# A two-layer encoder trunk on one core: seven products per couple of weight blocks in the mixers' output projections too, a fifth such couple in the down projections, and sums of weights formed by adding transfers

## The chip, the cores and the metric

The kernel runs on one core of one Trainium2 chip. The metric is the device time of one execution in microseconds (us); before the change it is 2400.95 us, the median of three runs (2400.9 to 2401.26).

## The reference, cut to what matters

All arrays are float32. A sequence of 256 tokens with 2048 features goes through two layers. Each layer adds a mixer's result to the residual stream `h`, and then that of a gated feed-forward part (ConvGLU); a last normalisation closes the trunk.

```python
for layer in range(2):
    hn = rmsnorm(h, norm_mix_g[layer])
    mix = mlstm_mixer(...) if layer == 0 else hgrn_mixer(...)   # each ends with:  y @ w_out   (2048 x 2048)
    h = h + mix
    h = h + conv_glu(rmsnorm(h, norm_ffn_g[layer]), ...)
return rmsnorm(h, final_g)

def conv_glu(hn, w_up, conv_w, conv_b, w_down):
    a, v = jnp.split(hn @ w_up, 2, axis=-1)      # w_up 2048 x 11008
    c = conv_b + depthwise convolution of width 3 of a
    return (gelu(c) * v) @ w_down                # w_down 5504 x 2048
```

What the change touches are the products with `w_out` (both mixers) and with `w_down` (both layers).

## The kernel before, in words

**Products in three terms.** A float32 weight block is split into a high part `wh`, cast by ScalarE (`parts`, L133), and a remainder `wl = raw - wh` by VectorE (L134); the tokens' factor is kept in two such parts as well. One block product is the sum of three matmuls: high by high, high by low, low by high. Each has 128 rows of the contraction and 512 columns, and accumulates into a bank of the matmuls' memory. Weights come in as tiles `raw` of 1 MB on SyncE's queue, three buffers deep; `stream` fetches pieces (`wh`, `wl`, 1024 columns) three ahead of their use (`LOOK`), with four buffers each (`WB`).

**Chunks.** The work is a list of `Chunk`s that TensorE takes one after another: "fm" chunks (up projections and the like), "tm" chunks (512 output columns, 16 or 21 contraction tiles, two banks of the pool `psm`, line L320), and "st" chunks (`squares_by_seven`, line L214), which cover 1024 output columns at once with four banks of `psm` (`mm`) and four of `psa` (`pc`).

**Seven products instead of eight.** An "st" chunk takes the contraction tiles two at a time: a unit, or couple, is a 2 x 2 grid of token blocks A (halves of the tokens by contraction tile) times a 2 x 2 grid of weight blocks B (contraction tile by columns): eight block products, 24 matmuls. For the units listed in `SEVEN = (1, 3, 5, 7)` a Winograd form is used with seven block products, 21 matmuls. It needs four sums of token blocks (`token_sums`, from tiles of the activations, kept as `sx`) and four sums of weight blocks: `combine` forms `T` (1024 columns wide, one VectorE instruction, L184) and `T_` (two instructions of 512, L186 and L187), then the high parts `th` (ScalarE, L189) and remainders `tl` (VectorE, L190). `T` and `T_` lie in the two buffers of the tag `avc`; `th` and `tl` have one buffer each. Four products of the seven read `th` and `tl`. When the last such unit is done, `mid` distributes the shared partial products to `h` (`hm`); at the chunk's end `done` adds the four `pc` banks.

**Where st chunks stand.** Each layer's feed-forward part has two parts of 22 and 21 contraction tiles. The first part ends with two st chunks (columns 0 to 1023, then 1024 to 2047), the second with one st chunk and two tm chunks. That makes three st chunks a layer, six in all, with four units of seven products each. The mixers' output projections are four tm chunks each (`project`, c = 0 to 3).

**Order.** A scheduler fixes every engine's order when the kernel is built, so matmuls of one unit may stand between those of another. Small jobs (transposes, head computations) are queued in `side` and are emitted as the matmuls tick by. `Norm.turn` transposes finished columns of `hm` for the next normalisation; it takes banks of `psa`. At the start TensorE runs 56 matmuls on ones (`idle`, L1096) while the first transfers are under way.

Of the kernel before, what the change touches and what calls it, by code (L numbers as in the profile page):

```python
# [20 lines left out]
FA = 22  # L21
# [24 lines left out]
LEAD = 48  # L46
GATES = 4 * AH
SEVEN = (1, 3, 5, 7)

QUAD = 32  # L50
# [6 lines left out]
def trunk_kernel(ctx, tc, xT, x_d, fg_d, pp_d, cst_d, w_gate, w_first, w_aq, w_ak, w_av, w_ao, w_aout,  # L57
                 w_bq, w_bv, w_bg, w_bout, w_up, w_d0, w_d1, w_d2, out, mscr):
# [53 lines left out]
    side = Side()  # L112
# [56 lines left out]
    def split_squares(ch, parts):  # L169

        units, raws, sums = (ch.nk + 1) // 2, {}, {}

        def raw(u):
            if u not in raws and u < units:
                raws[u] = load_raw(ch.src, 2048 * u, min(2048 * (u + 1), 1024 * ch.nk))
            return raws.get(u)

        def combine(u):
# [5 lines left out]
            dve.tensor_tensor(T.rearrange("p (a b) -> p a b", a=2), B12.unsqueeze(1).broadcast_to([P, 2, 512]),  # L184
                              r[:, 0:1024].rearrange("p (a b) -> p a b", a=2), ALU.subtract)
            dve.tensor_tensor(T_[:, 0:512], B22, T[:, 0:512], ALU.subtract)  # L186
            dve.tensor_tensor(T_[:, 512:1024], B21, T_[:, 0:512], ALU.subtract)  # L187
            for c, t in ((slice(0, 1024), T), (slice(1024, 2048), T_)):
                act.copy(th[:, c], t)  # L189
                dve.tensor_tensor(tl[:, c], t, th[:, c].bitcast(F32), ALU.subtract)  # L190
# [12 lines left out]

    def squares_by_seven(ch, fetch, ready):
# [4 lines left out]
        begun = set()  # L209

# [13 lines left out]
        for u in range(units):  # L224
# [26 lines left out]
            for ps, (x, w), (y, v) in ((C11, (A11, B11), (A12, B21)), (C12, (A11, B12), (A12, B22)),  # L251
                                       (C21, (A21, B11), (A22, B21)), (C22, (A21, B12), (A22, B22))):
                product(ps, x, w, False)
                product(ps, y, v, end)
                side.tick(1.3)
        ch.done(psa_)
# [88 lines left out]
    class Norm:  # L345
# [26 lines left out]
        def turn(self, c):  # L372
            yield 2.5
            for k0 in (4 * c, 4 * c + 2):
                pz = aux("pz")
                for k in (k0, k0 + 1):
                    for t in range(2):
                        o = (k - k0) * T + t * P
                        pe.transpose(pz[:, o:o + P], hm[:, t, k * P:(k + 1) * P], ident)  # L379
                for k in (k0, k0 + 1):  # L380
                    self.take(k, pz[:, (k - k0) * T:(k - k0 + 1) * T])
                yield 1.0
            if c == 3:
                self.total()
                self.finish()
                self.spread()
# [108 lines left out]
    def slot(j, name, more=None):  # L495
        where = keep if j < KT else more
        return where.tile([P, 2 * T], F32R, tag=f"yt{j}", name=f"{name}{j}")


    def mlstm(norm, nxt):  # L500
# [273 lines left out]
        def end():  # L774
            side.drain()
            stack.close()

        tail = project(lambda c: w_aout[c], KT, yx, nxt)
        tail[1].before = end
        return chunks + tail  # L780


    def hgrn(norm, nxt):
# [197 lines left out]
        def end():  # L981
            side.drain()
            stack.close()

        tail = project(lambda c: w_bout[c], KT, yx, nxt)
        tail[1].before = end
        return chunks + tail


    def ffn(layer, norm, nxt):  # L990
# [11 lines left out]

        def token_sums(u, a, b, S, SX):

            sx = box["mp"].tile([P, 1024], F32R, tag=f"sx{SEVEN.index(u)}", name="sx")
            for i, (x, y, op) in enumerate(((a[:, P:T], b[:, P:T], ALU.add), (a[:, P:T], a[:, 0:P], ALU.subtract),
                                            (S[:, 0:P], a[:, 0:P], ALU.subtract), (b[:, 0:P], S[:, 2 * P:3 * P], ALU.subtract))):
                dve.tensor_tensor(S[:, i * P:(i + 1) * P], x, y, op)
            act.copy(sx[:, 0:512], S)
            dve.tensor_tensor(sx[:, 512:1024], S, sx[:, 0:512].bitcast(F32), ALU.subtract)  # L1010
            SX[u] = sx

        def pair(src, nk, q, GT, SX, norm):

            u = []

            def part(t, c):
                o = 1024 * q + 512 * c
                return hm[:, t, o:o + 512]

            def mid(ps):
                P1, P6, P7, P5 = ps
                u2, u3 = (box["mp"].tile([P, 512], F32, tag=n, name=n) for n in ("u2", "u3"))
                act.copy(u2, P1)
                dve.tensor_tensor(part(0, 0), part(0, 0), P1, ALU.add)
                dve.tensor_tensor(u2, u2, P6, ALU.add)
                dve.tensor_tensor(u3, u2, P7, ALU.add)  # L1027
                dve.tensor_tensor(part(1, 1), part(1, 1), P5, ALU.add)
                dve.tensor_tensor(u2, u2, P5, ALU.add)
                pool.tensor_tensor(part(1, 0), part(1, 0), u3, ALU.add)  # L1030
                pool.tensor_tensor(part(1, 1), part(1, 1), u3, ALU.add)
                pool.tensor_tensor(part(0, 1), part(0, 1), u2, ALU.add)

            def done(ps):
                for i in range(4):
                    h = part(i // 2, i % 2)
                    dve.tensor_tensor(h, h, ps[i], ALU.add)
                if norm is not None:
                    norm.add(2 * q)
                    side.push(second())  # L1040

            def second():
                yield 3.0
                norm.add(2 * q + 1)

            ch = Chunk("st", src, nk, lambda k: GT[k], done)
            ch.mid, ch.seven, ch.sums = mid, SEVEN, lambda u: SX[u]
            pairs.append(ch)
            return ch

        def done_up(f, i, GT, SX):
            def go(ps):
# [15 lines left out]
                if i % 2 and i // 2 in SEVEN:  # L1068
                    token_sums(i // 2, box["c"], c, avc[:, 0:2 * T], SX)
# [3 lines left out]
        for part, (f0, nf) in enumerate(((0, FA), (FA, FB))):  # L1073
            GT, SX = [], {}
            for i in range(nf):
                chunks.append(Chunk("fm", w_up[layer, f0 + i], KT, norm.x, done_up(f0 + i, i, GT, SX),
                                    begin if f0 + i == 0 else None,
                                    swap=(1 + (layer == 0),) if part and i == 0 else ()))
            chunks.append(pair(w_d0[layer][:, f0 * 1024:(f0 + nf) * 1024], nf, 0, GT, SX, nxt if part else None))
# [4 lines left out]
            else:  # L1084
                chunks.append(pair(w_d1[layer], nf, 1, GT, SX, None))
# [8 lines left out]
    for i in range(56):  # L1094
        o = i % 4 * QUAD
        pe.matmul(idle[o:o + QUAD, 0:86], ones[:, 0:QUAD], ones[:, 0:86], start=True, stop=True)  # L1096
# [46 lines left out]
def layout(x, norm_mix_g, norm_ffn_g, mlstm_w_in, mlstm_b_gate, mlstm_head_g, mlstm_w_out, hgrn_w_in, hgrn_lb,  # L1143
# [8 lines left out]
    def squares(q, n):  # L1152

        v = down[:, :n, :, 2 * q:2 * q + 2]
        m = n // 2
        w = v[:, :2 * m].reshape(2, m, 2, P, 2, 512)
        w = np.stack([w[:, :, 0, :, 0], w[:, :, 1, :, 1], w[:, :, 1, :, 0], w[:, :, 0, :, 1]], axis=3)
        w = w.transpose(0, 2, 1, 3, 4).reshape(2, P, m * 2048)
        return np.ascontiguousarray(np.concatenate([w, v[:, 2 * m:].transpose(0, 2, 1, 3, 4).reshape(2, P, -1)], axis=2))

    up = A(ffn_w_up).reshape(2, KT, P, 2, FT, P).transpose(0, 4, 2, 1, 3, 5)
# [14 lines left out]
        w_aout=_cols(A(mlstm_w_out)[0], 512),  # L1176
        w_bq=_cols(qfb, 256),
        w_bv=_cols(wb[:, 2048:4096], 512), w_bg=_cols(wb[:, 4096:6144], 512),
        w_bout=_cols(A(hgrn_w_out)[0], 512),
        w_up=np.ascontiguousarray(up).reshape(2, FT, P, KT * 256),  # L1180
        w_d0=squares(0, FT), w_d1=squares(1, FA),
# [4 lines left out]
def build(nc, ins, out_shape=(2, P, D), **kw):  # L1186
# [4 lines left out]
    with tile.TileContext(nc, schedule_with_timeline_sim=True) as tc:  # L1191
        with ExitStack() as ctx:
            trunk_kernel(ctx, tc, ap["xT"], ap["x"], ap["fg"], ap["pp"], ap["cst"], ap["w_gate"], ap["w_first"],
                         ap["w_aq"], ap["w_ak"], ap["w_av"],
                         ap["w_ao"], ap["w_aout"], ap["w_bq"], ap["w_bv"], ap["w_bg"],
                         ap["w_bout"], ap["w_up"], ap["w_d0"], ap["w_d1"], ap["w_d2"], out, mscr, **kw)
# [12 lines left out]
```

## Time and profile before

| | |
|---|---|
| median of three runs | 2400.95 us (2400.9 to 2401.26) |
| profiled execution, its own time | 2402.44 us |
| its span in the profile | 2400.6 us |
| TensorE (PE) busy | 2388.8 us, 14606 matmul records |
| VectorE (DVE) busy | 1829.0 us, 76% of the span |
| ScalarE (ACT) busy | 1260.8 us, 53% |
| GpSimd (POOL) busy | 185.5 us, 8% |
| bytes moved | 451.19 MB, mean 188 GB/s |

Matmuls overlap in the pipeline, so the mean duration of a record (389 ns) is longer than the distance from one to the next; the sums in the prediction go by the distance. A group's row gives busy time and mean of one instruction, then the idle time just before these instructions and what ended it.

### The profile page before, as it was taken

The page shows a single profiled execution, that of the slowest core. Times are in us where ns is not written, and L with a number is a line of the kernel's source. Part 1 is how long each engine was busy: PE and PEld are TensorE (multiplying, and loading weights), DVE is VectorE, ACT ScalarE, POOL GpSimd, SP SyncE. Part 2 cuts the span into 40 slices and gives each one's busy share as a digit, 9 for nine tenths or more (in the row PEclk, how much of TensorE's full clock was granted, in tenths as well). Part 3 has the DMA queues.
Part 4 walks back from the last instruction along what each step waited for, and adds up shares of the span by engine and source line. Part 5 has one row for each costly group of instructions (what it writes and reads, how often), then busy time and mean ns, then how long its engine had stood idle before and what let it go on. Part 6 is the DMA issues. An engine that isn't in the chain of part 4 may idle for free.

```text
span 2400.6 us, 37188 instructions
## 1 busy us (share of the span) xinstructions
PE 2388.8 (100%) x14606; PEld 2044.3 (85%) x14606; DVE 1829.0 (76%) x3009; ACT 1260.8 (53%) x1959; POOL 185.5 (8%) x242
## 2 busy tenths in 40 slices
PE   9999999999999999999999999999999999999998
PEld 7888888888888888888888888888888888888887
DVE  7766656777887777867898989885777788777784
ACT  7655455555544455555555555555555454444553
POOL 0100000000000000001222222210000000000000
PEclk9999999999999999999999999999999999999999
DMA  8654555555555555555555455545555555555654
GB/s 299 199 185 163 188 176 180 191 192 193 186 212 198 185 188 190 201 184 180 174 176 173 165 174 176 176 161 191 189 187 189 191 196 208 193 180 189 202 195 147
DMA packets 67679, 451.19 MB, mean 188 GB/s; under 512 B 7712, under 2 KB 8224, under 8 KB 15024
## 3 DMA queue, kind: packets, MB, share of 16 engines
q1 hardware_dynamic: 65520, 444.29, 54.4%
q0 software_dynamic: 1120, 3.21, 0.8%
q8 instruction: 114, 1.87, 0.3%
q10 hardware_dynamic: 864, 1.32, 0.2%
q14 instruction: 61, 0.50, 0.1%
HBM read 446.63 MB, written 2.16 MB: 187 GB/s over the span
## 4 chain that ended last, share of the span: by engine, by line
PE 99%; DMA 0%; issue 0%; ACT 0%; SPq 0%; DVE 0%; POOLq 0%; POOL 0%
PE mm L304 37%; PE mm L320 26%; PE mm L308 18%; PE pc L214 11%; PE mm L214 3%; PE pn L657 1%; PE py L921 1%; PE pd L871 0%; PE pz L379 0%; PE pa L871 0%; DMA raw<-in_w_first 0%; PE S L643 0%; PE pz L942 0%; PE pa L896 0%; PE pa L895 0%; PE pz L685 0%
## 5 line engine op out<-in xcount | busy, mean ns | idle before, releaser
L134 DVE TENSOR_TENSOR wl<-raw,wh 128x1024 fp32r<-128x1024 f32 (+1 forms) x846 | 1016.4, 1207 | 429.0 <-ACT wh L133 420.2
L304 PE MATMUL mm<-xt,wh 128*128 128x512 f32 x3776 | 1318.4, 395 | 0.0
L133 ACT CAST wh<-raw 128x1024 fp32r<-128x1024 f32 (+1 forms) x846 | 861.4, 1028 | 762.4 <-issue 260.2
L308 PE MATMUL mm<-xt,wl 128*128 128x256 f32 x3776 | 1049.2, 279 | 0.0
L304 PEld LDWEIGHTS mm<-xt,wh 128*128 128x128 f32 x3776 | 706.8, 188 | 162.3
L308 PEld LDWEIGHTS mm<-xt,wl 128*128 128x128 f32 x3776 | 710.3, 188 | 4.1 <-issue 0.4
L320 PE MATMUL mm<-wh,xt 128*128 128x512 f32 x1024 | 320.2, 391 | 2.0 <-ACT xt L326 1.1
L320 PEld LDWEIGHTS mm<-wh,xt 128*128 128x128 f32 x1024 | 191.5, 188 | 41.8 <-ACT xt L326 1.5
L214 PE MATMUL pc<-wh,g 128*128 128x512 f32 x704 | 225.2, 389 | 0.0
L320 PE MATMUL mm<-wl,xt 128*128 128x512 f32 x512 | 198.0, 391 | 0.0
L331 ACT COPY b<-mm 128x256 f32<-128x256 f32 x236 | 87.4, 370 | 158.8 <-PE mm L308 158.7
L214 PEld LDWEIGHTS pc<-wh,g 128*128 128x128 f32 x704 | 132.1, 188 | 27.5
L214 PE MATMUL pc<-wl,g 128*128 128x512 f32 x352 | 136.0, 389 | 0.0
L320 PEld LDWEIGHTS mm<-wl,xt 128*128 128x128 f32 x512 | 96.2, 188 | 18.9
L332 DVE TENSOR_TENSOR avc<-mm,b 128x256 f32<-128x256 f32 x172 | 72.0, 420 | 41.4 <-ACT b L331 41.3
L320 PE MATMUL mm<-wh,g 128*128 128x512 f32 x308 | 96.4, 391 | 0.0
L1030 POOL TENSOR_TENSOR hm<-hm,u 128x512 f32<-128x512 f32 x6 | 7.8, 1296 | 1015.5 <-DVE u L1027 1015.5
L320 PE MATMUL mm<-wh,yb 128*128 128x512 f32 x256 | 80.7, 393 | 0.0
L320 PE MATMUL mm<-wh,ya 128*128 128x512 f32 x256 | 80.6, 393 | 0.0
L214 PEld LDWEIGHTS pc<-wl,g 128*128 128x128 f32 x352 | 66.1, 188 | 13.6
L189 ACT CAST th<-T 128x1024 fp32r<-128x1024 f32 x48 | 49.1, 1052 | 48.7 <-DVE T L187 15.5
L337 DVE TENSOR_TENSOR avc<-avc,R 128x256 f32<-128x256 f32 x172 | 72.1, 421 | 2.8
(227 smaller groups left out, 2236.7 us busy)
## 6 DMA issues: line engine op xcount, KB each, us to landing
raw<-in_w_up SPq DMA_DIRECT2D x172, 1024.0 KB, 4.9
raw<-in_w_d SPq DMA_DIRECT2D x84, 1024.0 KB, 4.9
raw<-in_w_bq SPq DMA_DIRECT2D x48, 1024.0 KB, 5.0
raw<-in_w_ao SPq DMA_DIRECT2D x16, 1024.0 KB, 4.8
raw<-in_w_aout SPq DMA_DIRECT2D x16, 1024.0 KB, 4.8
raw<-in_w_bv SPq DMA_DIRECT2D x16, 1024.0 KB, 4.8
raw<-in_w_bg SPq DMA_DIRECT2D x16, 1024.0 KB, 4.8
raw<-in_w_bout SPq DMA_DIRECT2D x16, 1024.0 KB, 4.8
```

The costliest lines, as they stand in the source:

```text
L133: pin(act.copy(wh[:, :m], r))
L134: pin(dve.tensor_tensor(wl[:, :m], r, wh[:, :m].bitcast(F32), ALU.subtract))
L189: act.copy(th[:, c], t)
L214: pe.matmul(ps, a, b, start=id(ps) not in begun, stop=stop and i == 2)
L304: pe.matmul(ps[f], wh[:, c:c + P], x, start=k + kk == 0, stop=False)
L308: pe.matmul(ps[f][:, 0:T], wl[:, c:c + P], x[:, 0:T], start=False, stop=k + kk == ch.nk - 1)
L320: pe.matmul(ps[t], x[:, a + t * P:a + (t + 1) * P], w[:, c], start=st and i == 0, stop=sp and i == 2)
L331: act.copy(b, ps[:, T:2 * T])
L332: dve.tensor_tensor(dst, ps[:, 0:T], b, ALU.add)
L337: dve.tensor_tensor(dst, dst, R, ALU.mult)
L657: pe.matmul(pn[:, 0:258], w, v, start=(i == 0), stop=(i == len(parts) - 1))
L921: pe.matmul(py[:, c], AT[:, s if s == t else 2 + s], V[:, s, j * P:(j + 1) * P], start=(s == 0), stop=(s == 1))
```

## The change

- The mixers' output projections become three chunks instead of four: a tm chunk for columns 0 to 511, an st chunk for columns 512 to 1535 with units 2, 4 and 6 in seven products (`SEVEN_MIX`), and a tm chunk for the last 512 columns (`mixed`). The token sums of these units are formed by a job `token` that starts when the first chunk is done. The banks of `psa` are held by an st chunk, so a list `held` makes `Norm.turn` wait until it is over.
- The down projections' st chunks get a fifth unit of seven products: `SEVEN = (1, 3, 5, 7, 9)`.
- In the down projections the wide sum `T` is no longer formed by VectorE: `add_in_flight` has GpSimd's queue load 128 x 1024 into `T` and then add 128 x 512 into each half of it by two transfers that add to what is there. It is issued two units ahead. The signs of the sums are turned so that all of them are additions; `mid` loses the tiles `u2` and `u3`, uses the tile `jk` instead, and has six VectorE instructions and two of GpSimd where it had five and three.
- In the mixers (`late=True`) VectorE still forms `T`, and `combine` comes after the unit's first piece.
- The first `idle` matmuls are 65 of 74 columns instead of 56 of 86. The order of two matmuls at the start of the second feed-forward part is the same in both layers now (`swap`).
- The host lays out the middle columns of the output weights in squares (`outer`, `squares`).

```diff
-SEVEN = (1, 3, 5, 7)
+SEVEN = (1, 3, 5, 7, 9)
+SEVEN_MIX = (2, 4, 6)
...
+        def add_in_flight(u):
+
+            T, o = tile(), 2048 * u
+            pool.dma_start(T, ch.src[:, o:o + 1024])
+            for c in range(2):
+                pool.dma_start(T[:, 512 * c:512 * c + 512], ch.src[:, o + 1536:o + 2048], accum_op=ALU.add)
+            pre[u] = T
...
-            T, T_ = (ch.pool.tile([P, 1024], F32, tag="avc", bufs=2, name="T") for _ in range(2))
-            dve.tensor_tensor(T.rearrange("p (a b) -> p a b", a=2), B12.unsqueeze(1).broadcast_to([P, 2, 512]),
-                              r[:, 0:1024].rearrange("p (a b) -> p a b", a=2), ALU.subtract)
-            dve.tensor_tensor(T_[:, 0:512], B22, T[:, 0:512], ALU.subtract)
-            dve.tensor_tensor(T_[:, 512:1024], B21, T_[:, 0:512], ALU.subtract)
+            T = pre.pop(u, None)
+            if T is None:
+                T = tile()
+                dve.tensor_tensor(T.rearrange("p (a b) -> p a b", a=2), r[:, 0:1024].rearrange("p (a b) -> p a b", a=2),
+                                  B12.unsqueeze(1).broadcast_to([P, 2, 512]), ALU.add)
+            T_ = tile()
+            dve.tensor_tensor(T_[:, 0:512], B22, T[:, 0:512], ALU.add)
+            dve.tensor_tensor(T_[:, 512:1024], B21, T_[:, 0:512], ALU.add)
...
             r = raw(u)
-            if u + 1 in ch.seven:
-                combine(u + 1)
+            if not ch.late:
+                for v in (u + 1, u + 2) if u == 0 else (u + 2,):
+                    if v in ch.seven:
+                        add_in_flight(v)
+                if u + 1 in ch.seven:
+                    combine(u + 1)
             wh, wl = parts(r[:, 0:1024], 1024)
             yield wh, wl, 1
+            if u + 1 in ch.seven and ch.late:
+                combine(u + 1)
...
         def turn(self, c):
             yield 2.5
+            while held:
+                yield 1.0
...
+    def token_sums(mp, i, a, b, S):
+        sx = mp.tile([P, 1024], F32R, tag=f"sx{i}", name="sx")
+        ...
+        dve.tensor_tensor(S1, A22, A21, ALU.subtract)
+        dve.tensor_tensor(S3, A11, A21, ALU.subtract)
+        dve.scalar_tensor_tensor(S2, S1, -1.0, A11, ALU.mult, ALU.subtract)
+        dve.tensor_tensor(S4, A12, S2, ALU.add)
+        act.copy(sx[:, 0:512], S)
+        dve.tensor_tensor(sx[:, 512:1024], S, sx[:, 0:512].bitcast(F32), ALU.subtract)
...
+        def mid(ps):
+            P1, P6, P7, P5 = ps
+            u = ev.tile([P, 512], F32, tag="jk", bufs=1, name="u")
+            act.copy(u, P1)
+            dve.tensor_tensor(part(0, 0), part(0, 0), P1, ALU.add)
+            dve.tensor_tensor(u, u, P6, ALU.add)
+            dve.tensor_tensor(part(0, 1), part(0, 1), P5, ALU.subtract)
+            dve.tensor_tensor(part(0, 1), part(0, 1), u, ALU.subtract)
+            dve.tensor_tensor(part(1, 1), part(1, 1), P5, ALU.subtract)
+            dve.tensor_tensor(u, u, P7, ALU.add)
+            pool.tensor_tensor(part(1, 0), part(1, 0), u, ALU.add)
+            pool.tensor_tensor(part(1, 1), part(1, 1), u, ALU.subtract)
...
+    def mixed(w, w2, x, norm, close):
+
+        c0, _, _, c3 = project(lambda c: w[c // 3], KT, x, norm)
+        ...
+        two = pair(w2, KT, 1, x, sums, norm, SEVEN_MIX, True)
+
+        def token():
+            for i, u in enumerate(SEVEN_MIX):
+                f = two.pool.tile([P, 1024], F32, tag="avc", bufs=2, name="f")
+                for j in range(2):
+                    y = x(2 * u + j).bitcast(F32)
+                    dve.tensor_tensor(f[:, j * T:(j + 1) * T], y[:, 0:T], y[:, T:2 * T], ALU.add)
+                SX[u] = token_sums(two.pool, i, f[:, 0:T], f[:, T:2 * T], f[:, 2 * T:4 * T])
+                yield 5.0
+        ...
+        return [c0, two, c3]
...
-        tail = project(lambda c: w_aout[c], KT, yx, nxt)
-        tail[1].before = end
-        return chunks + tail
+        return chunks + mixed(w_aout, w_ao2, yx, nxt, stack.close)
...
-    for i in range(56):
+    for i in range(65):
         o = i % 4 * QUAD
-        pe.matmul(idle[o:o + QUAD, 0:86], ones[:, 0:QUAD], ones[:, 0:86], start=True, stop=True)
+        pe.matmul(idle[o:o + QUAD, 0:74], ones[:, 0:QUAD], ones[:, 0:74], start=True, stop=True)
```

More of the change, by code (lines that the diff above doesn't have):

```diff
@@ L255, in squares_by_seven @@
                 side.tick(1.3)
+        held.pop()
         ch.done(psa_)
@@ new lines, in pair, with part, done, second @@
+    def pair(src, nk, c0, x, sums, norm, seven, late=False):
+        def part(t, c):
+            o = 512 * (c0 + c)
+            return hm[:, t, o:o + 512]
+        def mid(ps):
[10 more added lines that the diff above has]
+            pool.tensor_tensor(part(1, 1), part(1, 1), u, ALU.subtract)
+        def done(ps):
+            for i in range(4):
+                h = part(i // 2, i % 2)
+                dve.tensor_tensor(h, h, ps[i], ALU.add)
+            if norm is not None:
+                norm.add(c0)
+                side.push(second())
+        def second():
+            yield 3.0
+            norm.add(c0 + 1)
+        ch = Chunk("st", src, nk, x, done)
+        ch.mid, ch.seven, ch.sums, ch.late = mid, seven, sums, late
+        return ch
@@ L979, in yx @@
             return YT[k]
[L981 to L987, printed above, removed]
+        return chunks + mixed(w_bout, w_bo2, yx, nxt, stack.close)
     def ffn(layer, norm, nxt):
@@ L1001, in begin @@
                 nxt.begin(box["mp"])
[L1003 to L1049, printed above, removed]
         def done_up(f, i, GT, SX):
@@ L1084, in ffn @@
             else:
-                chunks.append(pair(w_d1[layer], nf, 1, GT, SX, None))
+                chunks.append(two(w_d1[layer], 2, None))
         return chunks, stack.close
```

64 lines of the change are left out of this document (42 added, 22 removed).

## The prediction, made before the changed kernel was run

> **What bounds the kernel now.** I read the page's busy table and chain first, then the waits of TensorE, then the chain in order of time inside a down projection.
>
> ```profile
> PE 2388.8 (100%) x14606; PEld 2044.3 (85%) x14606; DVE 1829.0 (76%) x3009; ACT 1260.8 (53%) x1959; POOL 185.5 (8%) x242
> ...
> PE 99%; DMA 0%; issue 0%; ACT 0%; SPq 0%; DVE 0%; POOLq 0%; POOL 0%
> ```
>
> ```profile
> PE idle L1096 <- POOL ones L1089: 1.1, 1, 1.1
> PE mm L320 <- ACT xt L326: 1.1, 1, 1.1
> PE mm L320 <- ACT wh L133: 0.9, 1, 0.9
> ```
>
> TensorE is on the chain for 99% of the span, and it waits three times in all, 3.1 us, at the start. So a matmul that goes saves its full distance to the next one, and any wait that comes in costs its full length. The distance stands in a stretch of the chain (start, length, matmuls and weight loads as records of one line):
>
> ```profile
> 677.59 18.36 PE pc L214 x81
> ```
>
> 18.36 / 81 = 0.2267 us. A unit of eight products (24 matmuls) takes 5.44 us, one of seven (21) 4.76 us.
>
> The other engines are not idle around these stretches. The three st chunks of layer 0, then the mixer's second, third and fourth output chunks (columns: length, then PE, PEld, DVE, ACT, POOL busy, clock, share and rate of the transfer engines):
>
> ```profile
> 637.44:694.82 57.38, 57.38 (x254) 47.49 (x254) 50.97 (x59) 30.19 (x36) 3.80 (x3) 1.00 0.57 198
> 694.82:752.00 57.18, 57.18 (x254) 47.32 (x253) 45.84 (x50) 26.51 (x30) 3.80 (x3) 1.00 0.60 209
> 984.66:1039.07 54.41, 54.41 (x242) 45.06 (x241) 45.69 (x54) 27.88 (x34) 3.80 (x3) 1.00 0.56 197
> ```
>
> ```profile
> 330.40:352.20 21.80, 21.80 (x100) 18.01 (x99) 12.19 (x14) 10.33 (x14) 0.00 (x0) 1.00 0.52 178
> 352.20:374.00 21.80, 21.80 (x101) 18.03 (x100) 12.46 (x14) 11.23 (x16) 0.00 (x0) 1.00 0.53 174
> 374.00:396.00 22.00, 22.00 (x108) 18.42 (x108) 12.62 (x19) 11.23 (x16) 0.69 (x1) 1.00 0.55 182
> ```
>
> VectorE is 80 to 89% busy in the st chunks and 56% in the output chunks; the transfer engines are busy 0.52 to 0.60 of the time.
>
> **The matmuls that go.** One more unit in each of six st chunks and three in each of two mixers: 12 units, three matmuls fewer each, 36 x 0.2267 = 8.2 us. The built order of the changed kernel has just that: 36 matmuls of 512 columns fewer, nine more of `idle`, and all others, transposes too, in the old number. That is the whole gain to be had on the path: 2402.4 - 8.2 = 2394.2 us for the profiled execution (2400.6 of span and 1.8 around it), 2400.95 - 8.2 = 2392.8 for the median, which lies 1.5 below.
>
> **VectorE in the down projections.** Its forms, with mean ns of one behind the busy time:
>
> ```profile
> L134 DVE TENSOR_TENSOR wl<-raw,wh 128x1024 fp32r<-128x1024 f32 x802 | 987.2, 1236 | 420.7 <-ACT wh L133 412.3
> ...
> L190 DVE TENSOR_TENSOR tl<-T,th 128x1024 fp32r<-128x1024 f32 x48 | 57.4, 1219 | 4.2 <-ACT th L189 4.2
> ...
> L1063 DVE TENSOR_TENSOR avc<-avc 128x256 f32<-128x256 f32 x86 | 35.8, 416 | 1.0 <-ACT avc L1062 1.0
> ...
> L134 DVE TENSOR_TENSOR wl<-raw,wh 128x512 fp32r<-128x512 f32 x44 | 30.1, 686 | 8.3 <-ACT wh L133 7.9
> L184 DVE TENSOR_TENSOR T<-raw 128x1024 f32<-128x1024 f32 x24 | 29.3, 1219 | 3.8 <-DMA raw<-in_w_d 3.7
> ...
> L1008 DVE TENSOR_TENSOR avc<-avc 128x128 f32<-128x128 f32 x64 | 18.4, 287 | 1.1
> ...
> L186 DVE TENSOR_TENSOR T<-raw,T 128x512 f32<-128x512 f32 x24 | 16.5, 690 | 0.6
> ...
> L486 DVE TENSOR_TENSOR hm<-hm,mm 128x512 f32<-128x512 f32 x22 | 14.3, 681 | 4.1 <-PE mm L320 4.1
> ...
> L1010 DVE TENSOR_TENSOR sx<-avc,sx 128x512 fp32r<-128x512 f32 x16 | 10.9, 684 | 0.0
> ```
>
> ```profile
> L189 ACT CAST th<-T 128x1024 fp32r<-128x1024 f32 x48 | 49.1, 1052 | 48.7 <-DVE T L187 15.5 <-PE pc L214 13.4 <-issue 12.8
> ...
> L1024 ACT COPY u<-mm 128x512 f32<-128x512 f32 x6 | 3.5, 577 | 0.0
> ```
>
> A unit of seven cost VectorE 1.24 + 0.69 + 1.22 + 2 x 0.69 + 2 x 1.22 = 7.0 us before, against 2.5 for one of eight. A fifth on the old way adds 4.5 us to 51 of 57 and shortens the chunk by 0.7: it would not fit safely. Without the wide sum a unit costs 5.7: five are 28.7, six of eight are 14.8, `mid` and `done` ten times 0.68: 50.3 of 56.4 us. That fits about as before, so VectorE itself costs nothing; the cover is the pieces fetched three ahead (some 8 us of matmuls). `mid` now follows unit 9 instead of 7, with 2.7 us (21 tiles) or 5.4 us (22) of matmuls behind it; the next chunk wants the first two `mm` banks, free after one copy and two additions, 0.58 + 2 x 0.68 = 1.9 us. Nothing again; up to 1 us each of six times if VectorE is behind.
>
> **The chain of adding transfers.** This is the new thing, and no row shows an adding transfer. `T` keeps one buffer in the built order, and its next load waits for the remainder `tl` of the last `T`. So there is a loop: GpSimd issues the load of 512 KB, waits until it has landed, issues two adding transfers of 256 KB, these land, ScalarE casts, VectorE subtracts, and only then the next load is issued. Bounds for the transfers, median us from issue to landing at the end of a row, and behind them the four loads of the final gain (`fg`) on GpSimd's queue:
>
> ```profile
> raw<-in_w_d SPq DMA_DIRECT2D x84, 1024.0 KB, 4.9
> ...
> Mb<-mscr POOLq DMA_DIRECT2D x16, 128.0 KB, 6.1
> ...
> raw<-in_w_d SPq DMA_DIRECT2D x2, 512.0 KB, 4.8
> raw<-in_w_d SPq DMA_DIRECT2D x4, 256.0 KB, 2.7
> fg<-in_fg POOLq DMA_DIRECT2D x4, 256.0 KB, 6.6
> ```
>
> ```profile
> L431 POOL DMA_DIRECT2D fg<-in_fg x4: 536/538/616, 2270.0 to 2272.2; - x4
> ...
> DMA to landing us min/median/max: 3.7/6.6/7.7
> ```
>
> From below: SyncE's rows, 2.7 + 0.7 (1024 KB against 256 KB costs 2.2 more, so 0.7 for each further 256) + 2.7 + 0.5 for the second issue = 6.6 us. From above: the median of four queued transfers for each stage, 6.6 + 0.7 + 6.6 = 13.9. I take the nearest row, the shortest of GpSimd's 256 KB (3.7), since at most two stand in the queue: C = (3.7 + 0.7) + (3.7 + 0.5) = 8.6 us. The Trainium skill, "DMA: Bandwidth & Descriptors", section "Anatomy of one DMA", gives a GpSimd transfer 2.0 us plus its bytes at 436 GB/s: an estimate of 3.2 + 0.5 + 2.6 = 6.3 us for C, by which the loop would never be late; the row of 3.7 us where that rule says 2.6 makes me distrust it.
>
> The loop then takes C, 1.05 for the cast, 1.22 for the remainder and some 0.5 for three handovers (estimate): C + 2.8 = 11.4 us. A unit of seven and one of eight give TensorE 10.2 us, so the loop loses 1.2 us a turn; what saves it is the lead. The built order places the first load of a chunk 20.5 pairs of up-projection matmuls ahead of the chunk, at 0.345 us a pair:
>
> ```profile
> 635.89 0.39 PE L304 MATMUL mm<-xt,wh 128*128 128x512 f32 x1
> ...
> 636.23 0.40 PE L304 MATMUL mm<-xt,wh 128*128 128x512 f32 x1
> ```
>
> 7.1 us. From the chunk's start its end cannot come before -7.1 + 4 (C + 2.8) + C + 5.0 (the narrow sums 1.4, cast, remainder, and the last two products 1.4) = 5C + 9.1 = 52.1 us. TensorE's own work is 6 x 24 + 5 x 21 = 249 matmuls, 56.4 us, with 22 tiles, and 237, 53.7 us, with 21. For the two chunks in a row, whose loop runs on without a new lead, it is 10C + 23.1 = 109.1 against 112.9. All fit, with 1.6 to 4.3 us to spare, and the built order already pulls matmuls of later units ahead of the four products that wait. The loop decides from C = 9.0 on; each us more costs 10 + 5 a layer, 30 us in all. Two GpSimd instructions of `mid` stand behind a waiting adding transfer on that queue, and VectorE's `done` waits for them; as long as C holds, that is hidden in the last unit. In bytes a chunk goes from 11 MB to 16: 0.57 x 16 / 11 = 0.83 of the transfer engines.
>
> **The mixers.** The two chunks that become one had VectorE at 24.7 of 43.6 us. The st chunk has 183 matmuls, 41.5 us, and VectorE does 13 x 1.24 + 3 x 0.69 of pieces, 3 x 5.0 of weight sums (the wide one stays here), 3 x (2 x 0.42 + 4 x 0.29 + 0.68) = 8.0 of token sums: 41.3 us. Up to unit 2's four products (12.9 us in) it has 1.4 (`h`), 5.4 (two token sums), 5.0 and 3.2 of pieces: 15 us. Three pieces lie ready and the order puts unit 3's matmuls first, so I take 0.8 us of wait for each mixer, 1.6 in all; nothing if VectorE's issue overlaps well, 3 each if not. `Norm.turn` of three chunks moves into the last one, where VectorE then has some 21 of 21.8 us; the cover is the three pieces, 8 us of matmuls of the following up projection.
>
> **The start.** The idle matmuls end at 4.7 us, the first real one starts at 5.6:
>
> ```profile
> 1.10 3.63 PE L1096 MATMUL idle<-ones 128*32 128x86 f32 x112 [1.10 <-POOL ones L1089]
> ...
> 5.63 1.19 PE L320 MATMUL mm<-wh,xt 128*128 128x512 f32 x4 [0.91 <-ACT wh L133]
> ```
>
> Nine more at the same distance end at 5.3 even if fewer columns save nothing. That is free, as is the swapped pair.
>
> **Sum.** -8.2 + 1.6 = -6.6: 2395.8 us for a profiled execution, 2394.4 for the median.
>
> **Rivals.**
>
> *The loop is late (slower).* For it: GpSimd's transfers have medians of 6.1 and 6.6, not 3.7; an adding transfer must read its target too; `raw` keeps the engines busy more than half the time. Against it: the shortest rows have no other transfer of their queue ahead, as here. With C = 10: 123.1 against 112.9 and 59.1 against 53.7, 15.6 us a layer, 31.2 in all: 2400.95 - 8.2 + 31.2 = 2424 us. It decides against the change from C = 9.0 + 8.2 / 30 = 9.3 on. The Trainium skill, "SBUF — State Buffer", section "Who interferes with whom", has a rule that speaks for this rival: descriptors of GpSimd's transfers cannot be written while VectorE runs an instruction that takes both its ports; by the same section additions and subtractions of two tensors do not, and the forms above are of that kind.
>
> *The transfer engines are full (slower).* If an adding transfer occupies them three times as long as a plain one, a chunk needs (11 + 2.5 + 7.5) / 11 x 0.57 = 1.09 of its time: 9% of 166.5 us a layer, 30 in two: 2423 us. It decides from the point where the share passes 1, at 2.2 times. The share of 0.57 leaves it unlikely.
>
> *VectorE is late in the mixers (no change).* 3 us at each mixer and 1 us at six ends of st chunks take back 12: 2400.95 - 8.2 + 12 = 2405 at worst, half of it 2399. For it: 15 us of work against 12.9. Against it: VectorE had 43% to spare just before.
>
> *The change does not do what it says:* excluded by the count of matmuls in the built order.
>
> **Chances and range.** The forecast 0.52 (own range 2392 to 2396), the loop 0.30, full engines 0.05, mixers 0.13, of it 0.02 slower. 0.2% is 4.8 us, about what a measurement of this kernel can tell from no change; C between 8.9 and 9.3 falls inside it. Faster 0.53, same 0.13, slower 0.34. The range goes from the full gain with a margin for the start, 2391.5, to 2430, the loop at C = 10.2; beyond that, to the far bound of C (13.9, some 140 us more), lies not much over one case in ten.
>
> **What would show it.** Right: no idle time before the products on `th` and `tl`, VectorE's wait for `T` short, three transfers of `T` landing within 9 us, TensorE's sum down by 8 us. Wrong: TensorE waiting for `th`, `tl` or pieces behind them in the st chunks, most in the second of the two in a row; the loop's period over 12 us; landings of `raw` well over 4.9 us.

## The result, and the profile after

| | before | after |
|---|---|---|
| median | 2400.93 us (2400.85 to 2401.26, 4 runs) | 2528.76 us (2523.76 to 2534.71, 4 runs) |
| ratio | | 1.0531, 95% interval 1.0519 to 1.0544 |
| profiled execution, its own time | 2402.44 us | 2534.71 us |
| its span | 2400.6 us | 2532.9 us |

The change makes the kernel 5.3% slower, where the forecast had it 0.3% faster. The page of after, busy times and chain:

```profile
PE 2444.6 (97%) x14588; PEld 2061.3 (81%) x14588; DVE 1883.2 (74%) x3119; ACT 1285.1 (51%) x1995; POOL 258.9 (10%) x330
...
PE 80%; DMA 13%; DVE 2%; issue 1%; ACT 1%; POOL 1%; SPq 0%; POOLq 0%; ACTq 0%; DVEq 0%
PE mm L327 34%; PE mm L343 21%; PE mm L331 17%; DMA T<-in_w_d 13%; PE pc L236 3%; PE mm L236 1%; DVE tl L205 1%; DVE wl L135 1%; ACT th L204 1%; PE pn L762 1%; PE py L1020 1%; POOL T L187 0%; PE pd L970 0%; PE pz L404 0%; PE pa L970 0%
```

TensorE was 99% of the chain; now the transfers into `T` are 13% of it. The waits of TensorE (us in total, times, longest):

```profile
PE mm L236 <- ACT th L204: 54.2, 23, 5.6
PE pc L236 <- DVE wl L135: 4.9, 7, 2.1
PE mm L331 <- DVE wl L135: 4.2, 2, 2.3
PE pc L236 <- ACT wh L134: 3.6, 7, 1.3
```

Of 78.4 us of waits in all, 54.2 are spent before products that need `th`, the high part of the sum that is formed in flight. One turn and the start of the next in the chain of waits of layer 0 (start, length, what):

```profile
629.52 3.85 DMA T<-in_w_d
...
633.66 0.78 POOL T L187
634.45 9.54 DMA T<-in_w_d
643.99 0.02 issue
...
644.09 1.06 ACT th L204
...
645.17 1.24 DVE tl L205
...
646.69 3.69 DMA T<-in_w_d
...
650.66 0.54 POOL T L187
651.21 9.89 DMA T<-in_w_d
```

This is the loop as the prediction drew it: load, two adding transfers, cast, remainder, next load. Its first stage takes 3.85 and 3.69 us, but the adding stage 9.54 and 9.89 us. The chain C, the time from the issue of a load of `T` to the landing of its last addition, is here 643.99 - 629.52 = 14.5 us, not 8.6. These first turns are among the longest: over all thirty chains C is 12.9 us in the mean, from 10.6 to 17.2. GpSimd's side, in the timeline of that engine, gives the period over the chunk:

```profile
629.52 0.59 POOL L185 DMA_DIRECT2D T<-in_w_d  x1 [235.40 <-DVE avc L355]
...
646.69 0.55 POOL L185 DMA_DIRECT2D T<-in_w_d  x1 [11.21 <-DVE tl L205]
...
711.83 0.56 POOL L185 DMA_DIRECT2D T<-in_w_d  x1 [8.17 <-DVE tl L205]
```

There are five turns from 629.52 to 711.83, 16.5 us each in the mean, against 10.2 us of matmuls.

Behind these waits TensorE runs at half its clock for a while (window, length, PE busy and records, granted clock, share and rate of the transfer engines):

```profile
655.00:658.00 3.00, 3.00 (x15) 1.00 1.10 275
658.00:661.00 3.00, 0.89 (x4) 1.00 0.62 238
661.00:664.00 3.00, 1.25 (x2) 0.72 0.00 0
664.00:667.00 3.00, 3.00 (x8) 0.50 0.60 168
667.00:670.00 3.00, 3.00 (x10) 0.64 1.03 381
```

And one thing lies outside the st chunks: the up projections have become slower. Matmuls of the line `mm<-xt,wh` in equal windows of layer 0, first of before, then of after:

```profile
420.00:600.00 180.00, 180.00 (x520) 1.00 0.58 192
```

```profile
420.00:600.00 180.00, 180.00 (x510) 1.00 0.56 185
```

TensorE is busy throughout at the full clock in both, and gets through 510 pairs instead of 520: 64 pairs (512 and 256 columns) take 22.61 us instead of 22.19, which is 353.3 ns a pair instead of 346.7. The account, from the start times of the same matmuls in both traces: start and both mixers -2.9 us; the six st chunks with what follows each +39.1 (two), +20.6, +40.1 (two) and +23.6; the slower pairs +11.9; together 132.3, the difference of the spans. Inside the st chunks the distances between matmuls hold 106.5 us above 0.2267 us each: 76.1 in 70 distances over 0.48 us (waits), 27.8 in 168 of 0.30 to 0.44 us (half clock), little else.

### The profile page after: what moved, and what is told of

The parts are those of the page before. It is cut to its first block, busy times and chain, and to the rows that moved or that the text cites. A ratio compares the mean times of both kernels' runs of the same rounds, so it can differ in the third digit from the quotient of the medians.

```text
span 2532.9 us, 37515 instructions
## 1 busy us (share of the span) xinstructions
PE 2444.6 (97%) x14588; PEld 2061.3 (81%) x14588; DVE 1883.2 (74%) x3119; ACT 1285.1 (51%) x1995; POOL 258.9 (10%) x330
## 4 chain that ended last, share of the span: by engine, by line
PE 80%; DMA 13%; DVE 2%; issue 1%; ACT 1%; POOL 1%; SPq 0%; POOLq 0%; ACTq 0%; DVEq 0%
PE mm L327 34%; PE mm L343 21%; PE mm L331 17%; DMA T<-in_w_d 13%; PE pc L236 3%; PE mm L236 1%; DVE tl L205 1%; DVE wl L135 1%; ACT th L204 1%; PE pn L762 1%; PE py L1020 1%; POOL T L187 0%; PE pd L970 0%; PE pz L404 0%; PE pa L970 0%
## 5 line engine op out<-in xcount | busy, mean ns | idle before, releaser
L327 PE MATMUL mm<-xt,wh 128*128 128x512 f32 x3776 | 1332.7, 398 | 0.9 <-ACT wh L134 0.9
L236 PE MATMUL pc<-wh,g 128*128 128x512 f32 x620 | 213.2, 405 | 4.0 <-ACT wh L134 3.6
L236 PEld LDWEIGHTS pc<-wh,g 128*128 128x128 f32 x620 | 120.8, 196 | 36.7 <-ACT wh L134 10.1
L204 ACT CAST th<-T 128x1024 fp32r<-128x1024 f32 x72 | 74.7, 1046 | 136.6 <-DMA T<-in_w_d 103.3
L236 PE MATMUL mm<-th,sx 128*128 128x512 f32 x216 | 90.7, 459 | 54.2 <-ACT th L204 54.2
L236 PE MATMUL pc<-wl,g 128*128 128x512 f32 x310 | 124.5, 402 | 4.9 <-DVE wl L135 4.9
L205 DVE TENSOR_TENSOR tl<-T,th 128x1024 fp32r<-128x1024 f32 x72 | 86.9, 1221 | 34.9 <-ACT th L204 34.9
L185 POOL DMA_DIRECT2D T<-in_w_d x30 | 16.7, 558 | 931.6 <-DVE avc L355 470.9
L236 PEld LDWEIGHTS mm<-th,sx 128*128 128x128 f32 x216 | 45.7, 220 | 71.5 <-ACT th L204 63.8
L201 DVE TENSOR_TENSOR T<-raw,T 128x512 f32<-128x512 f32 x36 | 24.9, 691 | 97.9 <-DMA T<-in_w_d 92.6
```

Of the source, the lines that this page charges most:

```text
L236: pe.matmul(ps, a, b, start=id(ps) not in begun, stop=stop and i == 2)
L327: pe.matmul(ps[f], wh[:, c:c + P], x, start=k + kk == 0, stop=False)
```

## Experiments

Three things had to be told apart: whether the time went with the loop, the traffic or the queues behind it; what the rest of the change does without transfers; and where the slower pairs come from.

**All but the transfers.** The whole change, with `T` formed by VectorE.

```diff
-                for v in (u + 1, u + 2) if u == 0 else (u + 2,):
-                    if v in ch.seven:
-                        add_in_flight(v)
```

> The whole change, but without adding transfers: VectorE forms all five wide sums of a chunk. Theory: the loop is gone, 36 matmuls fewer give 2392.8 us, and VectorE, with some 57 us of work in chunks of 56.4, makes TensorE wait 0 to 3 us a chunk: 2393 to 2410 us. Rival (the fifth couple itself, its order and the work of VectorE, is what costs): above 2450 us.

2408.63 us (2407.44 to 2409.82), ratio 1.003 (1.0018 to 1.0042). So 120 of the 128 us go with the adding transfers, and VectorE's sums stay in the theory's range (2393 to 2410). Some 8 of these 120 us are the pitch of the pairs, the distance from one pair to the next: in this run the up projections of both second feed-forward parts are fast, in after they are slow. Windows of the same length there, first of after, then of this run:

```profile
840.00:990.00 150.00, 150.00 (x425) 1.00 0.57 186
```

```profile
810.00:960.00 150.00, 150.00 (x434) 1.00 0.56 190
```

The order of the matmuls at the start of these stretches differs between the two kernels; the version with plain loads below has the order of after there, and is slow there too. The five units on VectorE cost more than they save: 9.3 us of excess distances in the st chunks against 4.1 us of matmuls.

**Plain loads in place of the adding ones** (same three transfers, same bytes from memory, no addition):

```diff
-                pool.dma_start(T[:, 512 * c:512 * c + 512], ch.src[:, o + 1536:o + 2048], accum_op=ALU.add)
+                pool.dma_start(T[:, 512 * c:512 * c + 512], ch.src[:, o + 1536:o + 2048])
```

> The changed kernel with the two adding transfers as plain loads of the same 256 KB, waits as they were: the addition in T is left out. Theory (latency of the loop, of which the adding is a part): a packet of 2 KB takes 84 instead of 178 ns and the first comes sooner, the second stage falls from some 7.5 to 5 us, a turn from 15.5 to 12.5 us: 2400 to 2440 us. Rival (transfer engines full, or any two stages on GpSimd's queue): above 2500 us. Rival (the adding alone, nothing of the loop): 2393 us.

2484.59 us (2482.25 to 2486.7), ratio 1.0346 (1.0331 to 1.0362): 44 us less than after, and between the ranges of the theory (up to 2440) and of the rival (from 2500). The issues of the two kernels, after first (KB each, median us to landing):

```profile
T<-in_w_d POOLq DMA_DIRECT2D x30, 512.0 KB, 4.2
T<-in_w_d POOLq DMA_DIRECT2D x60, 256.0 KB, 6.2
```

```profile
T<-in_w_d POOLq DMA_DIRECT2D x30, 512.0 KB, 4.8
T<-in_w_d POOLq DMA_DIRECT2D x60, 256.0 KB, 4.6
```

Adding costs 1.6 us of landing at the median, and 0.97 us of GpSimd for each issue instead of 0.54. But two thirds of the loss stays without any adding: two stages through one buffer are too long even with plain loads (loads of `T` at 629.01 and, five turns later, at 700.06: 14.2 us a turn).

**One stage.** Only the first load of `T` is left, the adding transfers are gone.

```diff
-            for c in range(2):
-                pool.dma_start(T[:, 512 * c:512 * c + 512], ch.src[:, o + 1536:o + 2048], accum_op=ALU.add)
```

> The changed kernel without its two adding transfers: T holds only what the one plain load of 512 KB brings (the wide addition is left out). The chain is one stage, about 4.5 us, and the loop 4.5 + 2.8 = 7.3 us against 10.2 us of matmuls for a unit of seven and one of eight, so it is never late. Theory (the loop's length is what costs): 2400 to 2412 us (the version with the five units on VectorE had 2408.6; slow pairs in up to four stretches against before are in that), waits of TensorE for th under 5 us. Rival (a wait for any transfer at the head of VectorE's queue costs, however short): 2440 us or more.

2407.16 us (2405.92 to 2409.41), ratio 1.0026 (1.0015 to 1.0037). One transfer of 4.9 us at the same place, in the same queues, brings no wait for `th`. Loop theory: as expected; the rival, that any wait for a transfer at the head of VectorE's queue costs tens of us, falls. But the fifth unit does not pay here either: the st chunks hold some 9 us of excess distances, 5.0 of them in waits for pieces and for `h`, where the version with four units and no transfers (below) has less than 1.

**Wider spacing.** Units 1, 4 and 7 only: a turn may take 15.6 us (4.76 + 2 x 5.44).

```diff
-SEVEN = (1, 3, 5, 7, 9)
+SEVEN = (1, 4, 7)
```

> The changed kernel with SEVEN = (1, 4, 7): three units of seven in a down projection, three units apart, sums still by adding transfers. Theory (one T buffer, a loop of some 14 to 15 us against the distance of two units, 10.2 us): at a distance of 15.6 us the loop fits, so 2400.9 - 4.1 (mixers) + 4.1 (one unit fewer in six chunks) = 2401 us, up to 2410 with leftover waits. Rival (each adding transfer costs a fixed amount): three fifths of the loss, about 2400 + 0.6 x 130 = 2480 us.

2443.28 us (2440.39 to 2444.1), ratio 1.0171 (1.0154 to 1.0188): between the two expectations, and in the range of neither. The chain had grown. One of its longer turns:

```profile
642.82 7.33 DMA T<-in_w_d
650.15 0.28 issue
650.43 0.54 POOL T L187
650.98 7.82 DMA T<-in_w_d
```

C is 16.0 us in this turn, 18.7 with the rest of the loop: late against 15.6. Over all 18 chains C is 14.2 us in the mean, 12.9 in after. What TensorE waits for is now not `th` but `wl` (13.6 of 24.1 us). VectorE's timeline shows why:

```profile
663.40 4.09 DVE L135 TENSOR_TENSOR wl<-raw,wh 128x512 fp32r<-128x512 f32 x4
672.70 0.69 DVE L201 TENSOR_TENSOR T<-raw,T 128x512 f32<-128x512 f32 x1 [5.21 <-DMA T<-in_w_d]
673.31 1.22 DVE L135 TENSOR_TENSOR wl<-raw,wh 128x1024 fp32r<-128x1024 f32 x1
```

VectorE sits 5.21 us before an addition that needs `T`, with a piece of ordinary weights right behind it.

**One buffer against two.** Units 1, 3 and 5, in two versions that differ in one line. In the first, `T` in flight stays as in after: it shares the two buffers of the tag `avc` with `T_` and so has one. In the second it has a tag of its own, with two buffers.

```diff
-            T, o = tile(), 2048 * u
+            T, o = ch.pool.tile([P, 1024], F32, tag="fly", bufs=2, name="T"), 2048 * u
```

> The same three units (1, 3, 5) with one buffer for T in flight. Theory (the loop through one buffer): two late turns in each of the six chunks, 13 to 17 + 2.8 against 10.2 us, less the lead of about 7 us at a chunk's start and with half clock behind the waits: 2440 to 2490 us, and at least 30 us above the version with two buffers. Rival (the second buffer is not what matters): within 10 us of the version with two.

> The changed kernel with three units of seven in each down-projection chunk (1, 3, 5; two buffers for five would not fit into SBUF) and a tile of its own for T in flight, with two buffers: the next load and its adding transfers start while T is still in use. Matmuls: 36 - 36 = 0 fewer than the version of the mixers alone less 18, so 4.1 us more than its 2403.2. Theory (the loop through the one buffer is what costs): a unit of seven and one of eight take 10.2 us, two buffers give a loop of 20.4 us for chains of 13 to 17: 2403 to 2415 us, waits of TensorE for th under 5 us. Rival (adding transfers cost wherever they run, or VectorE's queue stands behind T all the same): 2440 us or more, like the version with the wide spacing.

One buffer: 2442.43 us (2441.34 to 2445.79), ratio 1.0172 (1.0158 to 1.0186). Two: 2408.23 us (2403.75 to 2409.65), ratio 1.0023 (1.0013 to 1.0033). The first is at the low end of what was expected, the second in the middle. With two buffers all waits of TensorE are these:

```profile
PE idle L1145 <- POOL ones L1138: 1.1, 1, 1.1
PE mm L343 <- ACT xt L349: 0.5, 1, 0.5
PE pz L404 <- DVE xt L350: 0.5, 1, 0.5
PE mm L343 <- ACT wh L134: 0.4, 1, 0.4
```

The transfers themselves are no quicker (medians of 6.1 us for the loads and 7.7 for the adding ones), and all but four of the 18 chains run in or near the st chunks, where the transfer engines are busier than in after (0.69 and 0.74 over its first two st chunks):

```profile
632.00:690.00 58.00, 58.00 (x267) 1.00 0.78 252
```

So what costs is that a load has to wait for its target. The traffic of these chains, 18 instead of 30, costs TensorE no wait. The second version has more than a second buffer: `avc` serves the up projections too, and with a tag of its own the first two chains of each layer are issued some 270 us before their chunk. A tag of its own with one buffer was not run, nor were two buffers with five units (said above not to fit, which no run shows).

**Traffic that nobody reads.** The same transfers beside the mixers' version, into a tile without readers.

```diff
-SEVEN = (1, 3, 5, 7, 9)
+SEVEN = (1, 3, 5, 7)
...
-            T, o = tile(), 2048 * u
+            T, o = ch.pool.tile([P, 1024], F32, tag="fly", bufs=1, name="T"), 2048 * u
...
-            T = pre.pop(u, None)
+            T = None
```

> The version with the mixers alone (four units of seven in each down-projection chunk, the wide sum by VectorE), and beside it the load and the two adding transfers for each such unit, into a tile of their own that nobody reads: all the traffic, none of the waiting. Theory (the waiting for T costs, not the traffic): within 6 us of the version with the mixers alone, 2403 to 2409 us, no waits of TensorE over 3 us in all beyond the start. Rival (the traffic takes the weights' transfers their time: 4/5 of the changed kernel's adding transfers): pieces come late, 2430 us or more, waits of TensorE for wl and wh.

2405.51 us (2401.96 to 2416.03), ratio 1.0032 (1.0019 to 1.0045). This run tells nothing about traffic beside the st chunks: with no reader to hold them back, the transfers were issued earlier, from 364.5 us on, in the end of the mixers and in the up projections. Nor can its time be set against the mixers' version to within 6 us, as the up projections run at the fast pitch in all four stretches here. It shows something else. TensorE's longest wait is 5.4 us, in front of a product (`pr`) that hangs on a result of GpSimd, and that instruction stood behind two transfer issues that waited for a landing:

```profile
1684.60 5.79 DMA T<-in_w_d
...
1690.68 1.75 POOL T L187 x2
1692.43 0.75 POOL rc L418
...
1693.64 1.20 PE pr L428 x4
```

**The mixers alone.** Three chunks in each mixer, four units of seven in the down projections, no transfers into `T`.

```diff
-SEVEN = (1, 3, 5, 7, 9)
+SEVEN = (1, 3, 5, 7)
...
-                for v in (u + 1, u + 2) if u == 0 else (u + 2,):
-                    if v in ch.seven:
-                        add_in_flight(v)
```

> Only the mixers' part of the change: SEVEN back to (1, 3, 5, 7) and no adding transfers, so that VectorE forms the wide sum in the down projections as before. Theory (the loop of adding transfers is what costs): 18 matmuls fewer than before, 18 x 0.2267 = 4.1 us less, and no waits, as the changed kernel's trace shows none between 300 and 420 us: 2396.9 us, 2396 to 2398. Rival (VectorE late in the mixers and behind them): 2403 us or more.

2403.23 us (2402.05 to 2403.54), ratio 1.0006 (0.9997 to 1.0015): 6 us over what was expected, and in the range of the rival, VectorE late. But there are 1.5 us of waits in the whole kernel, so VectorE is not late; most of the 6 us is in the pairs. In 420 to 600 us it has 510 of them, as after has. By the times of single chunks (32 pairs), the first part of both layers takes 11.30 us a chunk instead of 11.09, 4.5 us a layer, and the second part of layer 1 takes 11.09 instead of 11.30, which gives back 4.2.

**One number in the kernel before.** In before, the slow pitch is in the last stretch, where `swap` has pair 1 instead of 2.

```diff
-                                    swap=(1 + (layer == 0),) if part and i == 0 else ()))
+                                    swap=(2,) if part and i == 0 else ()))
```

> The kernel before with one number changed: the exchanged pair in the first up-projection chunk of layer 1's second part is pair 2, as it is in layer 0, in place of pair 1. Nothing else. Theory (pitch of pairs): in the trace of before, 64 pairs of up-projection matmuls (512 and 256 columns) take 22.19 us in three of the four up-projection stretches and 22.61 us in the last; which of the two a stretch gets is settled by the order of the matmuls at its beginning and holds to its end. Pair 2 gave 22.19 us in layer 0 and in the two versions without adding transfers. Then the last stretch (about 670 pairs) is 4.4 us shorter: 2396.6 us, no wait of TensorE added. Rival (the pitch belongs to the place, to its neighbours or to the stage's other work): 2401 us, the last stretch still at 22.61.

2396.85 us (2395.88 to 2397.52, 11 runs), ratio 0.9981 (0.9973 to 0.999): 4.5 us less, as the pitch had it. The same window in before and in this kernel:

```profile
2080.00:2240.00 160.00, 160.00 (x454) 1.00 0.57 187
```

```profile
2080.00:2240.00 160.00, 160.00 (x463) 1.00 0.56 189
```

**A scan of exchanges** in the mixers' version, nine chunks in the first part of each layer.

```diff
+        scan = ({2: (2,), 4: (3,), 6: (4,), 8: (2,), 10: (3,), 12: (5,), 14: (1,), 16: (6,), 18: (10,)},
+                {2: (3,), 4: (4,), 6: (2,), 8: (5,), 10: (1,), 12: (6,), 14: (2,), 16: (10,), 18: (13,)})
...
-                                    swap=(2,) if part and i == 0 else ()))
+                                    swap=(2,) if part and i == 0 else () if part else scan[layer].get(i, ())))
```

> The version with the mixers alone (2403.2 us), with exchanged pairs in nine of the 22 up-projection chunks of the first part of each layer, at different places. There its 64 pairs took 22.61 us from the first chunk to the last, in both layers, where before had 22.19. Theory (pitch of pairs, settled by the order and kept): one of the exchanges brings the stretch to 22.19 and another may bring it back, so the trace shows both pitches with the changes just at the exchanges; if the fast one holds in most chunks, 2394 to 2398 us. Rival (the slow pitch comes from other work beside these chunks, for instance the mixer's additions that now lie later): 22.61 throughout, 2403 us.

2398.94 us (2397.73 to 2399.18), ratio 0.999 (0.9981 to 0.9999). In layer 0 every exchange turned the pitch: chunks 2 and 3, 6 and 7, 10 and 11, 14 and 15, and 18 to 20 took 11.09 to 11.16 us, the others from chunk 1 on 11.25 to 11.31. In layer 1 the exchanges at chunks 2, 8 and 18 left a slow stretch slow; those at 4, 10 and 14 made it fast, those at 6, 12 and 16 slow again. Between exchanges nothing changed.

**Mixers and pairs.** The scan's first exchanges alone.

```diff
+        scan = ({2: (2,)}, {2: (3,), 4: (4,)})
```

> The version with the mixers alone and exchanged pairs early in the first part of the up projection: chunk 2 of layer 0 (pair 2), chunks 2 and 4 of layer 1 (pairs 3 and 4), as they turned the slow pitch into the fast one in the scan. Theory: 19 chunks of layer 0 and 18 of layer 1 go from 11.30 to 11.09 us: 2403.2 - 7.8 = 2395.4 us, the fastest of all versions, 5.5 us under before. Rival (a later exchange or a stage between brings the slow pitch back): 2399 to 2403 us.

2394.86 us (2394.33 to 2397.12, 9 runs), ratio 0.9973 (0.9963 to 0.9983): 0.27% under before and 5.3% under after. It is the lowest time of all versions, though its interval overlaps that of the one number alone (0.9973 to 0.999).

## Why the prediction was wrong, step by step

- **What bounds the kernel, and the matmuls that go:** the count was right. There were 18 records fewer (36 matmuls fewer and nine `idle` more at two records each). But not all of the 8.2 us was to be had: in the two versions with five units and no late loop, the st chunks lose about 9 us where the fifth units save 4.1.
- **VectorE in the down projections:** "would not fit safely" held for the old way with five: it costs some 9 us, more than the 4.1 it saves. "VectorE itself costs nothing" without the wide sum did not show: the version with one stage, where VectorE is spared that sum, has some 9 us of excess too, and whether VectorE's work or the load of `T` brings them was not separated. And VectorE was not free of the transfers: a row of the changed kernel's groups has its additions idle for `T`.

```profile
L201 DVE TENSOR_TENSOR T<-raw,T 128x512 f32<-128x512 f32 x36 | 24.9, 691 | 97.9 <-DMA T<-in_w_d 92.6
```

- **The chain of adding transfers** is the step that failed. The mechanism, one loop through one `T`, was right; a term of C was far too small. C = (3.7 + 0.7) + (3.7 + 0.5) = 8.6 us was measured as 12.9 in the mean of thirty chains, near the far bound of 13.9, and 14.5 and 14.4 in the first two turns. The first stage, 4.4 as estimated, took 4.8 in the mean. The term that failed is the second stage, 3.7 + 0.5 = 4.2 us: it took 7.6 in the mean, from 6.0 to 10.4, the longest being the 0.78 + 9.54 and 0.54 + 9.89 shown above. The shortest row of a plain transfer was taken for an adding one. Instead, the adding transfers land after 6.2 us at the median, the second 1.5 us behind the first (3.8 in the turn at 650.66); each needs 0.97 us of GpSimd where 0.5 was taken; and they run beside `raw`. In the packets of the trace, 2 KB that are added take 178 ns at the median, 4 KB that are only loaded 159.
- **The price of "30 us per us of C"** holds for after: with C = 12.9 the formula gives 118 us and, with -8.2 for the matmuls and 12 for the pairs, 2523 us; 2529 was measured. With plain loads, C = 10.4, it gives 2448, and 2485 was measured. There the rest of the loop took 4.0 us in the mean of turns that follow each other, not 2.8, with pieces of ordinary weights in VectorE's queue between; 1.2 us more in each of the formula's 26 turns are some 30 of the missing 37 us. So the rival "the loop is late" was the right one; it was priced at C = 10, and a C near the far bound was held to be unlikely.
- The Trainium skill, "DMA: Bandwidth & Descriptors", section "Anatomy of one DMA", gave an estimate of 6.3 us for C. The trace has 12.9 in the mean, so the measurement decides. The same page says under "Issuing engines are not separate DMA queues" that transfers of all queues interleave on the same 16 engines. The landings fit it, plain loads of 256 KB taking from 2.9 to 6.3 us beside `raw`, but the traces do not tell which engine carried a packet.
- **The half clock** is in no step. In the st chunks 28 us of the excess are distances at half clock. Whether they add to the time was not tested: where the loop is late, a quicker TensorE would wait the longer, and the formula of the loop comes near the measured time without them. The Trainium skill, "TensorE: Matmul & The Clock Gate", section "HAM oscillation — how this bites in real kernels", tells of it: a wait for a transfer across a window of 3.4 us brings TensorE back at half rate. The trace agrees for the wait at 658 us, where 3.8 us lie between two matmuls. It shows it behind a shorter one too: at 784.3 TensorE waited 2.5 us within a distance of 2.8 from one matmul to the next. A distance of 2.45 at 691.8 us was not followed by it.

```profile
781.00:784.00 3.00, 2.84 (x13) 1.00 0.96 185
784.00:787.00 3.00, 0.50 (x1) 1.00 0.26 47
787.00:790.00 3.00, 2.89 (x12) 0.77 0.42 93
790.00:793.00 3.00, 3.00 (x13) 0.66 0.99 396
```

- **The mixers:** the 0.8 us of wait in each did not come; VectorE kept up. From the matmuls alone 4.1 us were due; by the times of the same matmuls the two stretches shrank by 2.0 and 1.5.
- **The start, and the swapped pair:** "that is free, as is the swapped pair" was wrong. The order of a few matmuls costs or saves 4.2 to 4.5 us a stretch. In the changed kernel all four stretches run at the slow pitch, in before one of four: 12 us, more than the whole gain that was forecast. The two first parts are slow in most versions of the changed kernel; the two second parts only in after and with plain loads, whose matmuls stand in another order there.
- **Full transfer engines:** not what cost the time; 0.78 of them were busy beside an undisturbed TensorE in the version with two buffers. But that is with three chains a chunk. By the same step from 0.57, five would make 0.92 (an estimate), more than the 0.83 of the prediction, and no run shows five chains without waits.

What stays open: why a pair of matmuls has two pitches, and what in the order before a stretch picks one. The scan shows that an exchange can turn it, not by which rule. That VectorE's and ScalarE's queues carry the lateness to other pieces is seen in the traces and was not tested by itself. Some 1 to 2 us of the mixers' gain are not accounted for. How much of the gain of the version with two buffers comes from the separate tag, and where the 9 us of the fifth units go, was not separated either.

## What to carry to other kernels

A transfer that replaces an instruction brings its latency into a loop if its target has one buffer: write down the loop (issue, landing, each further stage, use, release) and compare it with the time between two uses, with the longest landing that the queue shows beside other traffic and not the shortest. Where the loop was longer here, one stage fewer or a tag with two buffers took the waits away. Before crediting or blaming an edit for a few us, compare the pitch of the matmuls in stretches that it did not touch.

## What the runs showed of the hardware that was not expected

- Alternating matmuls of 512 and 256 columns, at full clock and without waits, run at 346.7 or 353.3 ns a pair for hundreds of pairs on end. An exchange of two neighbours can switch between them; in layer 1 of the scan three of nine did not.
- An adding transfer of 256 KB: 0.97 us of GpSimd to issue (plain 0.54), median landing 6.2 us (plain 4.6), and 178 ns for a packet of 2 KB (plain: 159 ns for one of 4 KB).
- The granted clock fell to one half behind distances of 2.4 to 3.1 us between two matmuls as well, not only behind longer ones, but not behind every one of them.
